# A fourth weight buffer, a planner that plans in rounds, and the odd pairs' activations turned by transfers

## The chip, the cores and the metric

The kernel runs on one core of one Trainium2 chip. The metric is the device time of one execution in microseconds (us). The engines are PE (TensorE), DVE (VectorE), ACT (ScalarE), POOL (GpSimd) and SP (SyncE), which here only issues transfers.

## The reference

A decoder trunk of two layers on 256 tokens of width 2048, in float32. Layer 0 is a retention layer, layer 1 latent attention; each is followed by a squared-ReLU MLP of inner width 8192. The change touches the MLPs.

```python
def sq_relu_mlp(h, w1, w2):
    return jnp.square(jax.nn.relu(h @ w1)) @ w2

for layer in range(DEPTH):
    if layer < N_A_LAYERS:
        x = x + retention(rms_norm(x, norm_mix[layer]), ...)
    else:
        ...
        x = x + mla_attention(rms_norm(x, norm_mix[layer]), ...)
    x = x + sq_relu_mlp(rms_norm(x, norm_mlp[layer]), mlp_w1[layer], mlp_w2[layer])
```

## The kernel before

**Products.** Each float32 operand is split into a high part in the type float32r and the rest, a low part. ACT casts the high part (wh), DVE subtracts for the low one (wl), and a product takes three matmuls: high by high, high by low, low by high. `gemm_pair` makes a 256 x 1024 block of output from chunks of 256 rows of weights, 1 MB each: SP loads a chunk into a buffer raw (tag "raw", three of them), `quad` splits it. A chunk is of one of two kinds. With eight block products it takes 24 matmuls and two splits of 1024 elements. With seven, the saving by sums of blocks, it takes 21, and DVE makes sums of weights (u) first and then splits of 1024, 512, 1024 and 1024 elements. Which chunks have seven stands in tuples such as ODD = (1, 3, 5, 7); chunks of one pair are numbered 0 to 7. The results stand in PSUM as c11, c12, c21, c22 and, for the seven kind, p1, p5, p6, p7; `pair_out` copies and adds them.

**The MLP.** In `mlp` the inner width is cut into four groups. A group has two up pairs p (even, then odd; names u_20 to u_27 and u_30 to u_37 are the chunks of pairs 2 and 3) and two down pairs (d_100 to d_107 and d_110 to d_117 in group 1). An up pair gives 1024 inner activations of 256 tokens, which a down pair needs with the inner width on the partitions: they must be turned. For an even pair `turn_by_dma` does it: ACT copies the 16-bit halves apart (hid_h), SP issues four transposing transfers for each 512 columns (hid_t), ACT copies the halves together (hid_u), squares and casts. For an odd pair, where STEPS holds None, `turn_on_pe` does it: PE transposes 128 x 128 blocks against the identity into PSUM (hid_tp), and ACT squares from there. The first four blocks of a down pair's eight come from the even pair, the last four (hid_30 to hid_33 in group 1) from the odd one. Three of the four groups' down results are added to memory by accumulating transfers that POOL issues (`to_home`, x_home or xh).

**The order.** Nothing is issued as it is written. `Plan` records every operation with its cost (`time`), takes due dates from the end backwards (`due_dates`), and `schedule` places the operations forwards, on each engine the ready one that is due first, with the buffers of each tag as a resource. Queues of an engine are in order: an instruction that waits holds up all behind it. All records go through one line, L421, so the trace tells operations apart by tiles.

Of the kernel before, what the change touches and what calls it, by code (L numbers as in the profile page):

```python
# [11 lines left out]
F32 = mybir.dt.float32  # L12
# [9 lines left out]

AHEAD = {"f2k": 25000, "act": 30000, "small": 60000}
COPY = {128: 160, 256: 269, 384: 370, 512: 490, 640: 625, 768: 735, 1024: 952}
SCALED = {64: 220, 128: 292, 256: 365, 384: 468, 512: 588, 1024: 1070}
# [97 lines left out]
class Plan:  # L125
# [60 lines left out]
    def time(self, op, outs, ins):  # L186
        engine, (_, method) = op.engine, op.method
        n = max(v.index.size for v in outs if isinstance(v, View)) if any(isinstance(v, View) for v in outs) else 0
        m = max([n] + [v.index.size for v in ins])
        op.moves = None  # L190
        if "dma" in method:
            size = max(n, m) * P * (2 if "transpose" in method else 4)
            issue = {"SP": 380, "ACT": 100, "POOL": 870}[engine]
            if "transpose" in method:
                issue = 1290
            rate, wait = (208, 3200) if op.kw.get("accum_op") is not None else (349, 3000 if engine == "POOL" else 1800)
            if "transpose" in method:
                rate, wait = 180, 2200
            op.moves = (size / rate, wait)
            return issue, issue  # L200
        if engine == "PE":
            if method == "matmul" and ins[0].dtype == F32:
                return 1.68 * n, 1.68 * n + 160
            cost = max(109, n / 2.4 + 13.5) if method == "matmul" else 109
            if method == "matmul" and ins[0].dtype == BF16:
                cost = 427
            return cost, cost + 165
        if engine == "DVE":
            base = 129 if method == "scalar_tensor_tensor" else 69
            return base + 1.0417 * m, base + 85 + 1.0417 * m  # L210
        if engine == "ACT":
            plain = method == "copy"
            cost = between(COPY if plain else SCALED, m)
            if plain and outs[0].dtype == U16 and m == 512:
                cost = 632
            if method == "activation" and op.kw.get("accum_out") is not None:
                return cost + 40, cost + 60
            return cost, cost + 115
        if op.kw.get("op") == ALU.pow:
            return 1050 + 75 * n, 1050 + 75 * n  # L220
        if method == "tensor_tensor":
            return 560 + 1.5 * m, 560 + 1.5 * m
        return 450 + 2.8 * m, 450 + 2.8 * m
# [28 lines left out]
            if not op.after:  # L252
                op.due = -whole

    def schedule(self):
        import heapq

        self.due_dates()
        free = dict.fromkeys(self.LATENCY, 0.0)
        server = 0.0  # L260
        waiting = {e: [] for e in free}
        ready = {e: [] for e in free}
        slots = {t: [(0.0, i) for i in range(b[0].bufs)] for t, b in self.tags.items()}
        turn, taken, held = ({t: k() for t in self.tags} for k in (int, set, set))
        chain = [op for op in self.ops if op.engine == "PE"]
        front = [0, False]
        blocked = {t: {} for t in self.tags}
        for op in self.ops:
            op.behind = {o for o in op.behind if o.number not in op.before}
            for other in op.behind:  # L270
                other.ahead.append(op)
            op.left, op.ready, op.start = len(op.before) + len(op.behind), 0.0, None
# [55 lines left out]
        while True:  # L328
            best = None
# [133 lines left out]
TURNED_Y = 7  # L463
TURNED_X = (0,1)
TURNED_CQ = (0,1)
STEPS = (((3,3,4),(3,4,5)),(None,None))
TURNS = ((0,1),(0,1))
SEVEN, LATE, ODD, HEAD = (3, 5, 7), (5, 7), (1, 3, 5, 7), (2, 4, 6, 7)
QUERY, FOUR = (3, 4, 6, 7), (3, 5, 6, 7)
# [18 lines left out]
def yoco(ctx: ExitStack, tc: tile.TileContext, a):  # L488
# [3 lines left out]
    psum = ctx.enter_context(tc.tile_pool(name="ps", bufs=1, space=PSUM))  # L492

    def f2k(shape, name, dtype=F32):
        return nc.tile(pool, [P, *shape], dtype, name, "f2k", 14)

    def small(w, name):
        return nc.tile(few, [P, w], F32, name, "small", 36)
# [182 lines left out]

    def stream(w, chunk, cols, name, use, done=None, before=None):

        raw = nc.tile(pool, [P, 2048], F32, f"{name}_raw", "raw", 3)
        if before is None:
            nc.sync.dma_start(raw[:, :cols], w[chunk])
        n = cols // 2
        for half in range(2):
            wh = nc.tile(pool, [P, 1024], F32R, f"{name}_wh{half}", "wh", 5)
            wl = nc.tile(pool, [P, 1024], F32R, f"{name}_wl{half}", "wl", 5)  # L690
            cuts = 1
            if before is not None:
                cuts = 1 if half and chunk else 2
                m = n // cuts
                for i in range(cuts):
                    lo = half * n + i * m
                    nc.sync.dma_start(raw[:, lo : lo + m], w[chunk][:, lo : lo + m])
                    if i == 0:
                        before(half)
            m = n // cuts  # L700
            for i in range(cuts):
                lo = half * n + i * m
                low_part[0] = split(wh[:, i * m : (i + 1) * m], wl[:, i * m : (i + 1) * m], raw[:, lo : lo + m])
            use(half, wh, wl)
            if half and done is not None:
                queue.append((clock[0] + 0.5, -1, done))
            tick(0.5)
# [47 lines left out]

    def quad(w, chunk, x, mm, name, split_ends=False):

        raw = nc.tile(pool, [P, 2048], F32, f"{name}_raw", "raw", 3)
        nc.sync.dma_start(raw, w[chunk])
        v, more = x  # L760

        def a(t, k):
            return [v[:, k, i, t * P : (t + 1) * P] for i in range(2)]

        def s(n):
            return [more[:, n // 2, i, n % 2 * P : (n % 2 + 1) * P] for i in range(2)]

        def parts(src, n, part):
            wh = nc.tile(pool, [P, 1024], F32R, f"{name}_wh{part}", "wh", 5)
            wl = nc.tile(pool, [P, 1024], F32R, f"{name}_wl{part}", "wl", 5)  # L770
            low_part[0] = split(wh[:, : n * 512], wl[:, : n * 512], src)
            return [[i[:, j * 512 : (j + 1) * 512] for i in (wh, wl)] for j in range(n)]

        if more is None:
            b11, b22 = parts(raw[:, 0:1024], 2, 0)
            if not split_ends:
                mm("c11", a(0, 0), b11)
                mm("c21", a(1, 0), b11)
                mm("c12", a(0, 1), b22)
                mm("c22", a(1, 1), b22)  # L780
            b12, b21 = parts(raw[:, 1024:], 2, 1)
            if split_ends:
                for key, ks in (("c11", ((0, 0, b11), (0, 1, b21))), ("c21", ((1, 0, b11), (1, 1, b21))),
                                ("c12", ((0, 1, b22), (0, 0, b12))), ("c22", ((1, 1, b22), (1, 0, b12)))):
                    for t, k, b in ks:
                        mm(key, a(t, k), b)
                return
            mm("c11", a(0, 1), b21)
            mm("c21", a(1, 1), b21)
            mm("c12", a(0, 0), b12)  # L790
            mm("c22", a(1, 0), b12)
            return
        u = [nc.tile(pool, [P, 2, 512], F32, f"{name}_u{i}", "us", 2) for i in range(2)]
        nc.vector.tensor_tensor(
            u[0], raw[:, 0:1024].rearrange("p (i n) -> p i n", i=2),
            raw[:, 1024:1536].unsqueeze(1).to_broadcast([P, 2, 512]), op=ALU.add,
        )
        nc.vector.tensor_tensor(u[1][:, 0], u[0][:, 0], raw[:, 512:1024], op=ALU.add)
        nc.vector.tensor_tensor(u[1][:, 1], u[1][:, 0], raw[:, 1536:], op=ALU.add)
        b11, b22 = parts(raw[:, 0:1024], 2, 0)  # L800
        mm("p1", a(0, 0), b11)
        mm("c12", s(3), b22)
        (b21,) = parts(raw[:, 1536:], 1, 1)
        mm("c11", a(0, 1), b21)
        u2, u4 = parts(u[1].rearrange("p i n -> p (i n)"), 2, 2)
        mm("c21", a(1, 1), u4)
        mm("p6", s(2), u2)
        u1, u3 = parts(u[0].rearrange("p i n -> p (i n)"), 2, 3)
        mm("p5", s(1), u1)
        mm("p7", s(0), u3)  # L810
# [485 lines left out]
    def mlp(layer, act, r, done):  # L1296
        w1, w2 = a[f"mlp_w1_{layer}"], a[f"mlp_w2_{layer}"]
        f0 = 0
        for gi, nf in enumerate(GROUPS):
# [46 lines left out]
            for p in range(f0 // 2, (f0 + nf) // 2):  # L1346
                seven = (ODD, ODD)[p % 2] if p else LATE
                gemm_pair(
                    w1, p * 8, act, [i in seven for i in range(8)], f"u{layer}_{p}", lambda c, p=p, up=up: up(c, p)
                )  # L1350
            if last:
                x_tiles(f"mlp{layer}")
            for p in range(2):
# [15 lines left out]
                    into_x(done, c, p, 1) if last else to_home(c, p)  # L1369

                kinds = [i in ((LATE if last else (SEVEN, ODD)[1]) if p else (SEVEN, ODD)[0]) for i in range(2 * nf)]
                gemm_pair(w2, p * 32 + 2 * f0, blocks, kinds, f"d{layer}_{gi}{p}", add)
            f0 += nf

    ss = square_sums(NB, "ss2")
# [379 lines left out]
```

## Time and profile before

| | us |
|---|---|
| median of 3 runs | 2434.55 (2434.27 to 2435.98) |
| profiled execution, whole | 2433.66 |
| its span | 2431.9 |
| PE busy in the span | 2415.1 |
| DVE busy | 2228.8 |
| ACT busy | 1764.0 |

The profile is one execution. A matmul's duration is its way through the array, and matmuls overlap: the distance between starts is what one costs PE. The same holds in a small way for DVE and ACT, where an operation starts a little before the one ahead of it ends. In the rows below, x with a number counts instructions, and names leave out buffer numbers: hid_tp stands for all transposes of hidden activations, u_wh and d_wh for the high parts of up and down weights.

### The profile page before, as it was taken

The page shows a single profiled execution, that of the slowest core. Times are in us where ns is not written, and L with a number is a line of the kernel's source. Part 1 is how long each engine was busy: PE and PEld are TensorE (multiplying, and loading weights), DVE is VectorE, ACT ScalarE, POOL GpSimd, SP SyncE. Part 2 cuts the span into 40 slices and gives each one's busy share as a digit, 9 for nine tenths or more (in the row PEclk, how much of TensorE's full clock was granted, in tenths as well). Part 3 has the DMA queues.
Part 4 walks back from the last instruction along what each step waited for, and adds up shares of the span by engine and source line. Part 5 has one row for each costly group of instructions (what it writes and reads, how often), then busy time and mean ns, then how long its engine had stood idle before and what let it go on. Part 6 is the DMA issues. An engine that isn't in the chain of part 4 may idle for free.

```text
span 2431.9 us, 31709 instructions
## 1 busy us (share of the span) xinstructions
PE 2415.1 (99%) x11342; PEld 2027.4 (83%) x11342; DVE 2228.8 (92%) x2959; ACT 1764.0 (73%) x2505; POOL 251.7 (10%) x287
## 2 busy tenths in 40 slices
PE   9999999999999999999999999999999999999998
PEld 7888888888888888888888888998888888888877
DVE  6899999988999999999999998777899999899999
ACT  6667666666687858769668879677878587596694
POOL 6510001000000010010110001110000100100100
PEclk9999999999999999999999999999999999999999
DMA  9566669656675697696896766545766986977984
GB/s 341 179 212 201 201 199 257 216 190 220 217 239 209 206 258 236 211 260 221 237 279 211 222 216 200 169 140 188 218 219 197 256 239 208 256 227 220 270 230 160
DMA packets 161151, 537.33 MB, mean 221 GB/s; under 512 B 78560, under 2 KB 79968, under 8 KB 107744
## 3 DMA queue, kind: packets, MB, share of 16 engines
q1 hardware_dynamic: 139600, 489.09, 60.9%
q0 software_dynamic: 21248, 46.15, 9.6%
q8 instruction: 89, 1.46, 0.2%
q14 instruction: 70, 0.57, 0.1%
q10 hardware_dynamic: 144, 0.05, 0.0%
HBM read 479.14 MB, written 39.85 MB: 213 GB/s over the span
## 4 chain that ended last, share of the span: by engine, by line
PE 76%; DVE 13%; ACT 5%; issue 4%; DMA 3%; SPq 0%; DVEq 0%; ACTq 0%
PE u_c L421 14%; PE d_c L421 12%; PE rp_c L421 8%; PE ro_c L421 5%; DVE d_wl L421 5%; PE u_p L421 4%; PE uq_acc L421 4%; PE rq_acc L421 4%; PE rk_acc L421 4%; PE d_p L421 3%; PE rp_p L421 3%; DVE d_u L421 2%; PE ku_acc L421 2%; DMA u_raw<-in_mlp_w 2%; DVE u_wl L421 2%
## 5 line engine op out<-in xcount | busy, mean ns | idle before, releaser
L421 PE MATMUL d_c<-d_wh,hid 128*128 128x512 f32 x1412 | 456.3, 390 | 0.0
L421 PE MATMUL u_c<-u_wh,n 128*128 128x512 f32 x1328 | 429.6, 389 | 0.0
L421 PEld LDWEIGHTS d_c<-d_wh,hid 128*128 128x128 f32 x1412 | 265.0, 188 | 54.6
L421 PEld LDWEIGHTS u_c<-u_wh,n 128*128 128x128 f32 x1328 | 249.3, 188 | 51.6
L421 DVE TENSOR_TENSOR d_wl<-d_raw,d_wh 128x1024 fp32r<-128x1024 f32 (+1 forms) x256 | 279.3, 1106 | 0.2 <-ACT d_wh L421 0.2
L421 ACT CAST u_wh<-u_raw 128x1024 fp32r<-128x1024 f32 (+1 forms) x256 | 236.6, 953 | 53.8 <-PE u_c L421 37.3
L421 PE MATMUL d_c<-d_wl,hid 128*128 128x512 f32 x706 | 274.8, 389 | 0.0
L421 DVE TENSOR_TENSOR u_wl<-u_raw,u_wh 128x1024 fp32r<-128x1024 f32 (+1 forms) x256 | 273.6, 1093 | 1.2 <-ACT u_wh L421 1.2
L421 PE MATMUL u_c<-u_wl,n 128*128 128x512 f32 x664 | 258.8, 390 | 2.6 <-DVE u_wl L421 2.5
L421 ACT CAST d_wh<-d_raw 128x1024 fp32r<-128x1024 f32 (+1 forms) x256 | 240.9, 967 | 19.9 <-PE d_c L421 8.0
L421 ACT CAST d_wh<-d_u 128x1024 fp32r<-128x1024 f32 x106 | 108.8, 1051 | 146.9 <-DVE d_u L421 139.4
L421 ACT CAST u_wh<-u_u 128x1024 fp32r<-128x1024 f32 x120 | 122.4, 1051 | 103.3 <-DVE u_u L421 93.5
L421 PE MATMUL rp_c<-rp_wh,a 128*128 128x512 f32 x560 | 180.8, 390 | 0.0
L421 PEld LDWEIGHTS d_c<-d_wl,hid 128*128 128x128 f32 x706 | 132.6, 188 | 27.2
L421 DVE TENSOR_TENSOR u_wl<-u_u,u_wh 128x1024 fp32r<-128x1024 f32 x120 | 143.1, 1219 | 12.3 <-ACT u_wh L421 12.3
L421 PEld LDWEIGHTS u_c<-u_wl,n 128*128 128x128 f32 x664 | 124.6, 188 | 30.0 <-DVE u_wl L421 4.3
L421 ACT CAST rp_wh<-rp_raw 128x1024 fp32r<-128x1024 f32 x112 | 103.7, 944 | 59.2 <-PE rp_c L421 33.4
L421 DVE TENSOR_TENSOR d_wl<-d_u,d_wh 128x1024 fp32r<-128x1024 f32 x106 | 126.9, 1218 | 14.5 <-ACT d_wh L421 14.3
L421 DVE TENSOR_TENSOR rp_wl<-rp_raw,rp_wh 128x1024 fp32r<-128x1024 f32 x112 | 119.4, 1092 | 6.3 <-ACT rp_wh L421 6.3
L421 PEld LDWEIGHTS rp_c<-rp_wh,a 128*128 128x128 f32 x560 | 105.1, 188 | 22.7 <-DVE rk_u L421 1.1
L421 PE MATMUL u_p<-u_wh,n_more 128*128 128x512 f32 x360 | 120.6, 389 | 0.0
L421 POOL DMA_DIRECT2D xh<-d_c x48 | 41.6, 866 | 736.8 <-DVE d_wl L421 536.1
(492 smaller groups left out, 6029.4 us busy)
## 6 DMA issues: line engine op xcount, KB each, us to landing
u_raw<-in_mlp_w SPq DMA_DIRECT2D x128, 1024.0 KB, 6.4
d_raw<-in_mlp_w SPq DMA_DIRECT2D x128, 1024.0 KB, 5.2
rp_raw<-in_ret_w_gv SPq DMA_DIRECT2D x56, 1024.0 KB, 5.1
ro_raw<-in_ret_w_out SPq DMA_DIRECT2D x32, 1024.0 KB, 5.1
uq_raw<-in_mla_w_uq SPq DMA_DIRECT2D x24, 768.0 KB, 4.1
rq_raw<-in_ret_w_qk SPq DMA_DIRECT2D x16, 1024.0 KB, 5.9
rk_raw<-in_ret_w_qk SPq DMA_DIRECT2D x16, 1024.0 KB, 4.9
xh<-d_c POOLq DMA_DIRECT2D x48, 256.0 KB, 6.2
```

Source lines behind the costliest of these rows:

```text
L421: op.made = fn(*(real(v) for v in op.args), **{k: real(v) for k, v in op.kw.items()})
```

## The change

Seven things change. The tag raw gets four buffers, f2k sixteen of 2 KB per partition; the room comes from the scratch for descriptors of POOL's transfers, which goes from 16 KB (the default) to 4 KB a partition. STEPS gives the odd pairs the even pairs' way, so `turn_on_pe` is not used any more. All up pairs take their chunks in the order 0 to 5, 7, 6, and the last one (6, of eight products) closes c11, c21, c12 and c22 one after another (`ends`). The planner's costs for transfers are longer. `schedule` runs the forward pass, now `forward`, up to six times; after each, `latest` computes new due dates from the end backwards with each engine's own order as a limit, and the plan with the earliest planned end is kept. At the start, buffers count as free 1 us earlier.

```diff
+ROUNDS = 6
-            rate, wait = (208, 3200) if op.kw.get("accum_op") is not None else (349, 3000 if engine == "POOL" else 1800)
+            rate, wait = (150, 3200) if op.kw.get("accum_op") is not None else (330, 2600)
             if "transpose" in method:
-                rate, wait = 180, 2200
+                rate, wait = 180, 3000
+    def latest(self):
...
+        while True:
...
+            op = heapq.heappop(ready[e])[2] if ready[e] else heapq.heappop(waiting[e])[3]
+            op.due = free[e] = min(limit[op], free[e] - op.cost)
...
     def schedule(self):
+        self.due_dates()
+        best = None
+        for _ in range(ROUNDS):
+            try:
+                self.forward()
...
+            end = max(op.end for op in self.ops)
+            if best is None or end < best[0]:
+                best = (end, [(op.start, [b.slot for b in op.new]) for op in self.ops])
+            self.latest()
...
-        slots = {t: [(0.0, i) for i in range(b[0].bufs)] for t, b in self.tags.items()}
+        slots = {t: [(-1000.0, i) for i in range(b[0].bufs)] for t, b in self.tags.items()}
...
-STEPS = (((3,3,4),(3,4,5)),(None,None))
+STEPS = (((3,3,4),(3,4,5)),((3,3,4),(3,4,5)))
...
-        return nc.tile(pool, [P, *shape], dtype, name, "f2k", 14)
+        return nc.tile(pool, [P, *shape], dtype, name, "f2k", 16)
...
-        raw = nc.tile(pool, [P, 2048], F32, f"{name}_raw", "raw", 3)
+        raw = nc.tile(pool, [P, 2048], F32, f"{name}_raw", "raw", 4)
...
-                    w1, p * 8, act, [i in seven for i in range(8)], f"u{layer}_{p}", lambda c, p=p, up=up: up(c, p)
+                    w1, p * 8, act, [i in seven for i in range(8)], f"u{layer}_{p}", lambda c, p=p, up=up: up(c, p),
+                    **(({"order": (0, 1, 2, 3, 4, 5, 7, 6), "ends": True}, {"order": (0, 1, 2, 3, 4, 5, 7, 6), "ends": True}))[p % 2],
...
-    nc = bacc.Bacc("TRN2", target_bir_lowering=False, num_devices=1)
+    nc = bacc.Bacc("TRN2", target_bir_lowering=False, num_devices=1, dynamic_dma_scratch_size=4096)
```

In all, PE has 128 operations fewer (the transposes); DVE and POOL have the same ones; ACT has 96 more, all copies (32 into halves, 64 out of them), and its 32 squares from PSUM become squares in place; SP has 64 transposing transfers more.

PE in group 1 of layer 0: the end of chunk d_100 and the start of d_101. Before:

```order
L421 MATMUL d_10_c_8962<-d_100_wl_8921,hid_20_8825 128x512
L421 MATMUL d_10_c_8962<-d_100_wh_8911,hid_20_8825 128x512
L421 MATMUL hid_30_tp<-cst,u_3_c_8918 128x128
L421 MATMUL hid_30_tp<-cst,u_3_c_8925 128x128
L421 MATMUL hid_30_tp<-cst,u_3_c_8918 128x128
L421 MATMUL hid_30_tp<-cst,u_3_c_8925 128x128
L421 MATMUL hid_31_tp<-cst,u_3_c_8918 128x128
L421 MATMUL hid_31_tp<-cst,u_3_c_8925 128x128
L421 MATMUL hid_31_tp<-cst,u_3_c_8918 128x128
L421 MATMUL hid_31_tp<-cst,u_3_c_8925 128x128
L421 MATMUL d_10_c_8939<-d_101_wh_8941,hid_21_8891 128x512
L421 MATMUL d_10_c_8939<-d_101_wl_8964,hid_21_8891 128x512
```

And after:

```order
L480 MATMUL d_10_c_8998<-d_100_wh_8912,hid_20_8800 128x512
L480 MATMUL d_10_c_8998<-d_100_wl_8934,hid_20_8800 128x512
L480 MATMUL d_10_c_8998<-d_100_wh_8912,hid_20_8800 128x512
L480 MATMUL d_10_c_8973<-d_101_wh_8926,hid_21_8804 128x512
L480 MATMUL d_10_c_8973<-d_101_wl_8964,hid_21_8804 128x512
```

The batch of eight transposes is gone; the matmuls around it stand as they stood.

SP at the same place, where the loads of weights and the transposing transfers share one queue. Before:

```order
L421 DMA u_36_raw<-in_mlp_w_0 128x2048
L421 DMA_TRANSPOSE hid_20_t_8705<-hid_20_h_8694 128x4x128
L421 DMA_TRANSPOSE hid_20_t_8705<-hid_20_h_8702 128x4x128
L421 DMA_TRANSPOSE hid_20_t_8730<-hid_20_h_8694 128x4x128
L421 DMA_TRANSPOSE hid_20_t_8730<-hid_20_h_8702 128x4x128
L421 DMA u_37_raw<-in_mlp_w_0 128x2048
L421 DMA d_100_raw<-in_mlp_w_0 128x2048
L421 DMA d_101_raw<-in_mlp_w_0 128x2048
L421 DMA_TRANSPOSE hid_21_t_8859<-hid_21_h_8847 128x4x128
L421 DMA_TRANSPOSE hid_21_t_8859<-hid_21_h_8856 128x4x128
L421 DMA d_102_raw<-in_mlp_w_0 128x2048
L421 DMA_TRANSPOSE hid_21_t_8885<-hid_21_h_8847 128x4x128
```

And after:

```order
L480 DMA d_100_raw<-in_mlp_w_0 128x2048
L480 DMA d_101_raw<-in_mlp_w_0 128x2048
L480 DMA d_102_raw<-in_mlp_w_0 128x2048
L480 DMA d_103_raw<-in_mlp_w_0 128x2048
L480 DMA d_104_raw<-in_mlp_w_0 128x2048
L480 DMA_TRANSPOSE hid_30_t_8996<-hid_30_h_8984 128x4x128
L480 DMA_TRANSPOSE hid_30_t_9011<-hid_30_h_8984 128x4x128
L480 DMA_TRANSPOSE hid_30_t_8996<-hid_30_h_9005 128x4x128
L480 DMA_TRANSPOSE hid_30_t_9011<-hid_30_h_9005 128x4x128
L480 DMA d_105_raw<-in_mlp_w_0 128x2048
L480 DMA d_106_raw<-in_mlp_w_0 128x2048
L480 DMA d_107_raw<-in_mlp_w_0 128x2048
```

The even pair's transfers (hid_20, hid_21) have moved ahead of d_100; the odd pair's (hid_30) stand between the loads d_104 and d_105.

ACT after, from the first copy of the odd pair into halves to the first copies out of them; before, nothing of the odd pair but its squares from hid_tp stood here:

```order
L480 COPY hid_30_h_8984<-u_3_c_8940 128x1024
L480 CAST d_101_wh_8993<-d_101_raw 128x1024
L480 COPY hid_30_h_9005<-u_3_c_8953 128x1024
L480 CAST d_102_wh_9015<-d_102_raw 128x1024
L480 CAST d_102_wh_9023<-d_102_raw 128x1024
L480 CAST d_103_wh_9032<-d_103_raw 128x1024
L480 CAST hid_23_more<-hid_23_sum 128x2x256
L480 CAST d_103_wh_9059<-d_103_raw 128x512
L480 COPY hid_30_u<-hid_30_t_8996 128x512
L480 COPY hid_31_u<-hid_30_t_8996 128x512
L480 ACTIVATE u_3_c_8967<-u_3_c_8967,n_r 128x512
L480 CAST d_103_wh_9083<-d_103_u_9002 128x1024
```

The copy hid_30_u waits for two of the transfers above, and the casts of d_103 behind it wait with it. The cast of hid_30, which PE needs for chunk d_104, stands eleven instructions further on.

## Rows read from the trace of the kernel before

**Rows 1.** The page's first part: busy us, share of the span, instructions by engine.
```profile
PE 2415.1 (99%) x11342; PEld 2027.4 (83%) x11342; DVE 2228.8 (92%) x2959; ACT 1764.0 (73%) x2505; POOL 251.7 (10%) x287
```

**Rows 2.** Windows: length, busy PE, PEld, DVE, ACT, POOL (x), PEclk, DMA share, GB/s.
```profile
885.31:1051.01 165.70, 165.70 (x740) 137.35 (x740) 159.82 (x188) 122.35 (x159) 13.82 (x17) 1.00 0.78 235
...
1921.81:2087.00 165.19, 164.12 (x731) 135.20 (x730) 158.27 (x187) 120.44 (x155) 13.73 (x16) 1.00 0.79 235
```

**Rows 3.** PE in time around a batch of transposes: start us, us, operation, out<-in.
```profile
806.26 0.39 PE L421 MATMUL d_c<-d_wh,hid 128*128 128x512 f32 x1
806.49 1.03 PE L421 MATMUL hid_tp<-cst,u_c 128*128 128x128 f32 x8
807.28 0.48 PE L421 MATMUL d_c<-d_wh,hid 128*128 128x512 f32 x1
807.60 0.40 PE L421 MATMUL d_c<-d_wl,hid 128*128 128x512 f32 x1
```

**Rows 4.** The page's groups by line and form: the transposes of the hidden activations.
```profile
L421 PE MATMUL hid_tp<-cst,u_c 128*128 128x128 f32 x128 | 17.5, 274 | 1.5 <-ACT u_c L421 1.5
```

**Rows 5.** What PE and its weight loads (PEld) waited for: us, times, longest.
```profile
PE u_c L421 <- DVE u_wl L421: 2.5, 2, 2.1
...
PEld u_c L421 <- DVE u_wl L421: 4.3, 4, 2.6
PEld hid_tp L421 <- ACT u_c L421: 2.9, 4, 1.2
```

**Rows 6.** The same for DVE and ACT, two of their waits in the up pairs.
```profile
ACT u_wh L421 <- PE u_c L421: 45.3, 58, 1.7
...
DVE u_u L421 <- DMA u_raw<-in_mlp_w: 12.4, 15, 2.2
```

**Rows 7.** The chain that ended last, near PE's longest wait: start us, us, what.
```profile
2308.42 7.59 DMA u_raw<-in_mlp_w
```

**Rows 8.** The same chain in layer 0: two chunks that follow each other.
```profile
885.31 5.44 PE u_c L421 x24
895.51 5.44 PE u_c L421 x24
```

**Rows 9.** Groups by line and form on ACT: busy, mean ns, idle before and releaser.
```profile
L421 ACT CAST d_wh<-d_u 128x1024 fp32r<-128x1024 f32 x106 | 108.8, 1051 | 146.9 <-DVE d_u L421 139.4 <-DVE hid_sum L421 5.2 <-PE d_c L421 1.8
...
L421 ACT COPY hid_u<-hid_t 128x512 uint16<-128x512 uint16 x64 | 48.7, 779 | 4.8 <-DMA hid_t<-hid_h 4.8
...
L421 ACT CAST d_wh<-d_raw 128x512 fp32r<-128x512 f32 x53 | 33.0, 623 | 0.3 <-PE d_c L421 0.3
...
L421 ACT COPY hid_h<-u_c 128x1024 uint16<-128x1024 uint16 x32 | 32.1, 1038 | 0.1
```

**Rows 10.** DMA issues: times, KB each, median us from issue to landing.
```profile
xh<-d_c POOLq DMA_DIRECT2D x48, 256.0 KB, 6.2
...
hid_t<-hid_h SPq DMA_TRANSPOSE x64, 3.4
...
y_t<-y_h SPq DMA_TRANSPOSE x28, 5.8
```

**Rows 11.** Busy time by windows around the start of a down pair, layer 0.
```profile
1112.00:1132.00 20.00, 20.00 (x90) 16.53 (x90) 19.03 (x24) 18.93 (x26) 0.00 (x0) 1.00 0.76 230
1132.00:1153.00 21.00, 21.00 (x102) 17.56 (x101) 20.48 (x29) 20.90 (x33) 0.00 (x0) 1.00 0.67 216
1153.00:1173.00 20.00, 20.00 (x90) 16.56 (x89) 20.00 (x28) 13.07 (x17) 0.00 (x0) 1.00 0.50 174
```

**Rows 12.** DVE's instructions in time, operations of 1024 elements in a row.
```profile
1007.60 2.36 DVE L421 TENSOR_TENSOR d_wl<-d_raw,d_wh 128x1024 fp32r<-128x1024 f32 x2
1009.87 1.22 DVE L421 TENSOR_TENSOR d_u<-d_raw 128x1024 f32<-128x1024 f32 x1
```

**Rows 13.** ACT's instructions in time, two casts in a row.
```profile
1054.44 2.00 ACT L421 CAST u_wh<-u_u 128x1024 fp32r<-128x1024 f32 x2 [1.68 <-DVE u_u L421]
```

**Rows 14.** SP's queue in time, four transposing transfers in a row.
```profile
1107.68 5.12 SPq L421 DMA_TRANSPOSE hid_t<-hid_h  x4
```

More of the change, by code (lines that the diff above doesn't have):

```diff
@@ L253, in due_dates @@
                 op.due = -whole
-    def schedule(self):
+    def latest(self):
+        import heapq
+        left = {op: len(op.after) for op in self.ops}
+        behind = {op: [] for op in self.ops}
+        limit, free = {}, dict.fromkeys(self.LATENCY, 0.0)
+        waiting = {e: [] for e in free}
+        ready = {e: [] for e in free}
+        for op in self.ops:
+            for other, finish in op.after:
+                behind[other].append((op, finish))
+            limit[op] = -(op.took if op.moves is None else op.cost + sum(op.moves))
+            if not op.after:
+                heapq.heappush(waiting[op.engine], (-limit[op], -op.start, op.number, op))
+        while True:
+            best = None
+            for e in free:
+                w, r = waiting[e], ready[e]
+                while w and -w[0][0] >= free[e] - w[0][3].cost:
+                    heapq.heappush(r, heapq.heappop(w)[1:])
+                at = free[e] if r else -w[0][0] if w else None
+                if at is not None and (best is None or at > best[0]):
+                    best = (at, e)
+            if best is None:
+                break
+            e = best[1]
+            op = heapq.heappop(ready[e])[2] if ready[e] else heapq.heappop(waiting[e])[3]
+            op.due = free[e] = min(limit[op], free[e] - op.cost)
+            for other, finish in behind[op]:
+                gap = other.cost
+                if finish and not other.engine == op.engine == "PE":
+                    gap = (other.took if other.moves is None else gap + sum(other.moves)) + self.LATENCY[op.engine]
+                limit[other] = min(limit[other], op.due - gap)
+                left[other] -= 1
+                if not left[other]:
+                    heapq.heappush(waiting[other.engine], (-limit[other], -other.start, other.number, other))
@@ new lines, in schedule @@
+    def schedule(self):
+        self.due_dates()
+        best = None
+        for _ in range(ROUNDS):
+            try:
+                self.forward()
+            except RuntimeError:
+                if best is None:
+                    raise
+                break
+            end = max(op.end for op in self.ops)
+            if best is None or end < best[0]:
+                best = (end, [(op.start, [b.slot for b in op.new]) for op in self.ops])
+            self.latest()
+        for op, (start, slots) in zip(self.ops, best[1]):
+            op.start = start
+            for buf, slot in zip(op.new, slots):
+                buf.slot = slot
+        return sorted(self.ops, key=lambda op: (op.start, op.number))
@@ L256, in schedule, with forward @@
+    def forward(self):
         import heapq
-        self.due_dates()
         free = dict.fromkeys(self.LATENCY, 0.0)
@@ L267, in schedule @@
         blocked = {t: {} for t in self.tags}
+        for op in self.ops:
+            op.ahead = []
         for op in self.ops:
@@ L1371, in mlp @@
                 kinds = [i in ((LATE if last else (SEVEN, ODD)[1]) if p else (SEVEN, ODD)[0]) for i in range(2 * nf)]
-                gemm_pair(w2, p * 32 + 2 * f0, blocks, kinds, f"d{layer}_{gi}{p}", add)
+                gemm_pair(w2, p * 32 + 2 * f0, blocks, kinds, f"d{layer}_{gi}{p}", add, **(({}, {}))[p % 2])
             f0 += nf
```

2 lines of the change are left out of this document (1 added, 1 removed).

## The prediction

> **What bounds the kernel now.** I read the page's first part, then a table by stage, then what PE itself waits for. In the first, PE is busy in 99% of the span, DVE in 92%, ACT in 73% [rows 1]. The table by stage shows one group of an MLP in each layer, about 165 us long, both at a granted clock of 1.00, the 2.4 GHz level: in layer 0 PE is busy for 165.70 of 165.70 us and DVE for 159.82; in layer 1 PE misses 1.1 us [rows 2]. So time goes down only where PE has fewer instructions or where one of its few waits goes, and DVE is close behind: 5.9 us of room in a group.
>
> **The 128 transposes that leave PE.** The hidden activations of the odd pairs (four a layer) are turned on PE, 16 a pair in two batches of eight. The reader should look at starts, not at durations: the batch starts at 806.49, 0.23 us after the matmul before it, the matmul after it at 807.28 and the next only at 807.60 [rows 3]. Up to 807.60 these are 1.11 us, of which one matmul's own step is 0.23: a batch costs 0.88 us, 0.11 a transpose. 16 batches: 14.1 us off PE. In the new order PE goes straight from chunk d_100 to d_101, and the counts of the other matmuls stay.
> The grouped row gives a transpose a mean duration of 274 ns [rows 4]. The Trainium skill (TensorE: Matmul & The Clock Gate, Part 4: PE-mode transpose) has about 275 ns for one inside a kernel, and the trace agrees on the duration. Taken as a cost, that would be 128 x 0.274 = 35 us; the starts show that the transposes overlap, so the sum goes by 14.1.
>
> **Waits that go with them.** Before its transposes PE waited for the scaled activations: 1.5 us on the matmul side [rows 4], 2.9 on the weight-load side [rows 5]. I take the middle, 2.2. The activations are now waited for by ACT and SP, and what is late next is the turned block (below).
>
> **The fourth weight buffer.** PE waited for u_wl for 2.5 us, 4.3 by its loads [rows 5]. The chain shows the origin of the largest: with three buffers a load is issued when DVE lets go of one, and lands 7.59 us later [rows 7]; DVE waited for u_raw 15 times, 12.4 us in all [rows 6]. With a fourth buffer a load is issued one chunk, about 5 us of PE, earlier: 5.44 us for a chunk of 24 matmuls, and 10.20 - 5.44 = 4.76 for one of 21 [rows 8]. 7.6 us of landing then fit into the lead. I take 3.4 us (the middle of 2.5 and 4.3), and that the 12.4 us come back as room on DVE. The bounds are 0 and 4.3.
> The smaller descriptor scratch I cost at nothing. POOL's accumulating transfers come in runs of eight, and one lands after 6.2 us [rows 10]. If each had to wait for the landing of the one before, a run would take 8 x 6.2 = 50 us, still within a group's 165; only f2k buffers are held longer, of which there are two more. Above nothing there is no price that reaches PE, below nothing neither.
>
> **What is added.** 64 transposing transfers on SP, and on ACT 32 copies into halves and 64 copies out of them: 32 x 1.038 + 64 x 0.779 = 83 us [rows 9], 10.4 a group. On ACT's total (122 of 165 us in a group, rows 2) that is hidden. The place where it may not be is the start of a down pair: there ACT is busy for 20.90 of 21 us already, and for 13 of 20 in the stretch behind [rows 11]. The new plan answers in two ways that the order shows: the even pair's transfers are issued ahead of the odd pair's last chunks, so that its copies are over before d_100; and every up pair now ends with chunk 6, of eight products, which closes its sums one after another, while the sums p are closed a chunk earlier.
> The step that must hold: hid_30, the odd pair's first block, is read by chunk d_104. From the end of u_36 PE works for 3 x 5.44 + 4.76 = 21.1 us on d_100 to d_103 [rows 8]. In that time ACT has, from the first hid_30_h to the cast of hid_30, 23 instructions in the new order: 8 casts of 1.05 us, 4 copies of 1.04, 4 of 0.78, and 7 more of 512 elements, all taken at the 0.62 of the cast of that size [rows 9]: 20.0 us by durations. Two casts in a row take 2.00 and not 2.10 [rows 13], so 22 overlaps of 0.1 make it 17.8. With 0.7 us ahead of it for the copy of the last sum it is 18.5 to 20.7 against 21.1.
> The wait inside it: between the second hid_30_h and the first copy out stand three casts of 1024 and two of 512, about 4.0 us with their overlaps. SP needs 5.12 us to issue four transposes [rows 14], so the third is issued some 0.6 us after that hid_30_h, and lands 3.4 us after issue [rows 10]: at 4.0, just in time. At the 5.8 us of the retention's y_t [rows 10] ACT would stand for 2.4 us, with the weight casts of d_103 and d_104 queued behind it, and DVE and PE behind those. Bounds a group: 0, and 20.7 + 2.4 - 21.1 = 2.0; over eight groups 0 to 16 us. hid_t's own row is the nearer one, so I take 0.4 a group, 3.4 us. SP's d_105 load stands behind the four transposes, 5.1 us late; three loads are ahead of it, so it is hidden; without the fourth buffer DVE would wait for it.
> The added transfers carry 128 KB each, 8.4 MB, under 2% of the bytes. They fall where the queues have room: a share of 0.67 and then 0.50 from the start of a down pair on [rows 11].
> The Trainium skill (DMA: Bandwidth & Descriptors, Specifications) asks for pieces of at least 512 B for line rate, and more short pieces speak against the change. The trace shows something of it, a share of 0.76 at 230 GB/s with transposes against 0.50 at 174 without [rows 11].
>
> **The sum.** The profiled execution took 2433.66 us, 1.8 around a span of 2431.9. 2433.66 - 14.1 - 2.2 - 3.4 + 3.4 = 2417.4. The median of the runs shown, 2434.55, is 0.9 above the profiled one: 2418.
>
> **Rivals.**
> *The turned block comes late (A).* Transfers land as the retention's do, and each down pair stalls for 1 to 2 us: 8 to 16 us instead of 3.4, so 2423 to 2431. For it speaks an ACT almost without a gap at that place today [rows 11]; against it the 3.4 us of hid_t's landing, and that ACT waited for hid_t for only 4.8 us in all 64 copies [rows 9].
> *Two sevens in a row starve PE (B, slower).* The up pairs now end with chunks 5, 7, 6, of which 5 and 7 are of the seven-product kind. For such a chunk DVE does four operations of 1024 and three of 512 elements; two of 1024 are followed by the next after 2.27 us, a step of 1.14 [rows 12], and a 512 is estimated at half of it: 6.3 us of DVE against 4.76 of PE. Alternating, each deficit of 1.5 is made up by the next eight-product chunk (2.3 against 5.44); in a row it is 3.0, and the stock must cover it. If it is not there, each of 16 up pairs loses 1.5 us more: 24 us, so 2418 - 3.4 + 24 = 2439. It decides from 1.2 us a pair on. Against it: ACT found all its high-part buffers full 58 times in the up pairs, waiting for PE [rows 6], so there is a stock of five half chunks; and DVE gets the 12.4 us of rows 6 back.
> *Only the transposes count (C).* The buffer brings nothing and the new waits eat the rest: 2434.55 - 14.1 = 2420, within the forecast's own range.
> *More comes out (D).* No new wait at all, and the re-planned retention part loses its few waits too: 2434.55 - 14.1 - 2.9 - 4.3, and 1 to 3 for those waits: 2410 to 2412.
>
> **How the numbers follow.** The forecast with C, 2412 to 2423: 0.62. D, below 2412: 0.10. A, 2423 to 2431: 0.18. B: 0.10. A measurement of this kernel tells a change of 0.2%, 4.9 us, from none, so faster ends at 2429.7. A gives 0.12 to faster and 0.06 to the same; B, whose price runs from nothing to 24, 0.03 to the same and 0.07 to slower. That is 0.84, 0.09 and 0.07; for a mishap in the re-planned rest of the kernel, which I cannot price, I move 0.02 from faster to the other two: 0.82, 0.10 and 0.08. The range that holds 8 of 10 reaches from D's middle to most of A: 2409 to 2430.
>
> **What the new profile would show.** No hid_tp on PE, and 11,214 matmuls or so. hid_t with 128 transfers at about 3.4 us. In a group of layer 0 PE busy throughout, and a group of about 164 us instead of 165.7. DVE's wait for u_raw far under 12.4 us. The step on ACT is wrong if PE or DVE wait for a d_wh or hid cast at d_103 to d_105; B is right if PE waits for u_wl in chunks 7 and 6. I am wrong altogether if PE's idle time grows by more than 14 us.

## The result, and the profile after

The changed kernel takes 2447.5 us (median of 4 runs, 2446.3 to 2449.9), the kernel before 2435.3 beside it: ratio 1.0044, 95% interval 1.0031 to 1.0057. It is slower by about 12 us, where 2418 was forecast.

Page of the changed kernel, first part (busy us, share of the span, instructions), beside [rows 1]:

```profile
span 2445.5 us, 31624 instructions
PE 2426.7 (99%) x11214; PEld 2016.6 (82%) x11214; DVE 2247.5 (92%) x2959; ACT 1843.0 (75%) x2601; POOL 262.7 (11%) x287
```

The 128 transposes are gone from PE, ACT has 79 us more, and the span is 13.6 us longer. The first place to look is a stretch in which PE never stops. Windows of the changed kernel (columns as in [rows 2]; a line of dots stands for lines left out):

```profile
885.31:1051.01 165.70, 165.70 (x725) 135.70 (x724) 161.98 (x190) 132.35 (x171) 13.84 (x16) 1.00 0.85 241
...
800.00:1000.00 200.00, 200.00 (x873) 163.69 (x873) 194.57 (x231) 167.41 (x222) 13.89 (x16) 1.00 0.84 241
...
1112.00:1132.00 20.00, 20.00 (x88) 16.35 (x88) 19.82 (x24) 19.77 (x27) 0.00 (x0) 1.00 0.80 235
1258.00:1281.00 23.00, 21.15 (x93) 16.95 (x91) 15.99 (x21) 13.56 (x18) 2.81 (x6) 1.00 1.14 276
...
1281.50:1286.00 4.50, 3.66 (x9) 2.68 (x10) 4.40 (x5) 4.50 (x7) 0.00 (x0) 0.67 0.98 350
```

In the first row's 165.70 us the kernel before did 740 matmuls, 16 of them transposes [rows 2]; now 725 matmuls without a transpose fill the same 165.70 us, at the same granted clock of 1.00. So a group is not shorter, though work left it and PE did not wait. The second row says why: 200 us without idle time hold 873 matmuls, 229 ns each. Call the distance from the start of a matmul to the start of PE's next instruction its step. Worked out from the starts of all 512-column matmuls with steps under 300 ns, the mean step was 227.4 ns before (9331 steps) and is 229.9 now (9336). That is 9336 x 2.48 = 23.2 us, spread over the whole span.

What PE, DVE and ACT wait for in the changed kernel (us in total, times, longest), beside [rows 5, 6]:

```profile
PE d_c L480 <- ACT hid L480: 3.1, 2, 2.3
PE u_c L480 <- DVE u_wl L480: 2.9, 4, 0.8
PE u_c L480 <- ACT u_wh L480: 2.4, 1, 2.4
...
ACT hid_u L480 <- DMA hid_t<-hid_h: 12.9, 3, 7.7
```

DVE's 12.4 us for u_raw [rows 6] do not occur any more. In their place ACT stands for turned blocks for 12.9 us (4.8 before, [rows 9]), 7.7 us in one piece, and PE has waits for ACT that [rows 5] did not show. DMA issues of the changed kernel (count, KB, median us to landing), beside [rows 10]; the kernel before had for x_mlp, the tiles of x that the last groups read back, the row under it:

```profile
xh<-d_c POOLq DMA_DIRECT2D x48, 256.0 KB, 5.8
x_mlp<-xh POOLq DMA_DIRECT2D x16, 256.0 KB, 12.8
hid_t<-hid_h SPq DMA_TRANSPOSE x128, 3.8
```

```profile
x_mlp<-xh POOLq DMA_DIRECT2D x16, 256.0 KB, 4.9
```

The landing of all hid_t, before and after:

```profile
DMA to landing us min/median/max: 2.4/3.4/6.9
```

```profile
DMA to landing us min/median/max: 2.4/3.8/13.1
```

The median of hid_t has hardly moved; its longest landing has, from 6.9 to 13.1 us. The longest ACT wait lies in layer 0's last group. Timelines of the changed kernel, ACT and then PE (start us, us, what, idle time before and its releaser):

```profile
1271.17 1.04 ACT L480 COPY hid_h<-u_c 128x1024 uint16<-128x1024 uint16 x1
1279.87 0.76 ACT L480 COPY hid_u<-hid_t 128x512 uint16<-128x512 uint16 x1 [7.65 <-DMA hid_t<-hid_h]
1280.50 1.98 ACT L480 CAST u_wh<-u_u 128x1024 fp32r<-128x1024 f32 x2
```

```profile
1278.52 0.39 PE L480 MATMUL u_c<-u_wl,n 128*128 128x512 f32 x1
1278.75 0.40 PE L480 MATMUL u_c<-u_wh,n 128*128 128x512 f32 x1
1281.58 0.50 PE L480 MATMUL u_c<-u_wh,n 128*128 128x512 f32 x1 [2.44 <-ACT u_wh L480]
1282.84 0.67 PE L480 MATMUL u_c<-u_wl,n 128*128 128x512 f32 x1 [0.76 <-DVE u_wl L480]
1283.31 0.63 PE L480 MATMUL u_c<-u_wh,n 128*128 128x512 f32 x1
1283.74 0.63 PE L480 MATMUL u_p<-u_wh,n_more 128*128 128x512 f32 x1
```

ACT stands at the copy of a turned block; the weight cast behind it comes 7.65 us late, DVE's low part after it, PE stops for 2.44 and 0.76 us. Then the matmuls start 0.43 us apart instead of 0.23: the window 1281.5 to 1286 above has a granted clock of 0.67, between the 2.4 GHz level that PE had before it stood and 1.2 GHz; by 1287 it is 1.00 again.

By starts, first matmul to last: 128-column matmuls -15.2 us, 512-column steps under 300 ns +24.3 (23.2 by their length, 1.1 for five more of them), steps of 300 ns and more (the stalls) +4.6, the rest, shorter matmuls, +1.2: +15 us in all. The stalls are thus the smaller part.

### The profile page after: what moved, and what is told of

The parts are those of the page before. It is cut to its first block, busy times and chain, and to the rows that moved or that the text cites. A ratio compares the mean times of both kernels' runs of the same rounds, so it can differ in the third digit from the quotient of the medians.

```text
span 2445.5 us, 31624 instructions
## 1 busy us (share of the span) xinstructions
PE 2426.7 (99%) x11214; PEld 2016.6 (82%) x11214; DVE 2247.5 (92%) x2959; ACT 1843.0 (75%) x2601; POOL 262.7 (11%) x287
## 4 chain that ended last, share of the span: by engine, by line
PE 89%; ACT 4%; DVE 3%; DMA 2%; issue 1%; POOL 0%; SPq 0%; ACTq 0%; DVEq 0%; POOLq 0%
PE d_c L480 20%; PE u_c L480 17%; PE rp_c L480 9%; PE u_p L480 6%; PE d_p L480 6%; PE ro_c L480 6%; PE uq_acc L480 4%; PE rq_acc L480 3%; PE rk_acc L480 3%; PE rp_p L480 3%; PE ku_acc L480 2%; PE wo_acc L480 1%; PE ro_p L480 1%; PE dqp_c L480 1%; PE dq_acc L480 1%
```

## The experiments

**Where tiles lie.** The new plan moves more than the instructions the diff speaks of. SP issues the load of the table cst at 0.7 us before and at 12.3 us now:

```profile
L421 SPq DMA_DIRECT2D cst<-in_cst x1: 400/400/400, 0.7 to 0.7; - x1
```

```profile
L480 SPq DMA_DIRECT2D cst<-in_cst x1: 328/328/328, 12.3 to 12.3; - x1
```

The trace holds no addresses; those below are worked out from the programs. Tiles get their addresses in SBUF, the memory on the chip, in the order in which the plan first uses them. cst takes 2688 bytes of a partition, 10 x 256 + 128. Before, it lies ahead of all rings, and every weight and activation tile begins 192 bytes past a multiple of 256. Now three raw buffers, the first weight buffers wh0, wl0 and wh1, and an activation tile lie ahead of it and begin at 64; the others behind it at 192. The steps of the changed kernel go by buffer: products from wh0/wl0 take 232.2 ns, from the last two pairs of weight buffers under 229.

*cst first.* The changed kernel, same plan, with two tiles created before the others:

```diff
     with self.tc.manual_schedule(engines=engines):
+        for v in self.first:            # gains, cst
+            v.get()
```

> The changed kernel, with one tile (the table cst, 2688 B per partition) placed in SBUF ahead of the others again, as it lies in the kernel before; no instruction and no order changes, only addresses: every weight tile then begins 192 bytes past a multiple of 256, where in the changed kernel wh0, wl0 and wh1 begin 64 past one. Theory P (placement): the 512-column matmuls go back from 229.9 to about 227 ns from start to start, 9336 x 2.5 ns = 23 us less: 2424 us, ratio to the kernel before about 0.9955. Rival T (the added transposing transfers and ScalarE copies slow TensorE's reads everywhere): nothing changes, 2447 us, ratio 1.004.

2430.7 us, ratio to the kernel before 0.9966 (95% interval 0.9954 to 0.9977; so in all runs below). 882 matmuls in the same 200 us, 226.8 ns each. Windows of this run:

```profile
800.00:1000.00 200.00, 200.00 (x882) 164.95 (x882) 196.00 (x237) 168.29 (x223) 13.89 (x16) 1.00 0.83 239
```

By ratio it is 19 us faster than the changed kernel, between the profiled spans 16, and not 23: its stalls (of each step over 1.4 times the median of its size, what lies above the median, all added) are 40.1 us against 31.1. With the same plan, a faster PE waits longer for the others. Theory P holds, T falls.

*The mixture in the kernel before.* The first buffers of each ring, up to the second wh, are created ahead of cst in the kernel before:

```diff
     with self.tc.manual_schedule(engines=engines):
+        self.first[0].get()             # gains
+        seen = set()
+        for op in order:
+            for buf in op.new:
+                if buf.tag in ("raw", "f2k", "act", "wh", "wl", "us", "junk") \
+                        and (buf.tag, buf.slot) not in seen \
+                        and sum(t == "wh" for t, _ in seen) < 2:
+                    seen.add((buf.tag, buf.slot))
+                    buf.get()
```

> The kernel before, with the first buffers of the ring tags placed ahead of the table cst, up to the second wh buffer, so that wh0, wl0 and wh1 begin 64 bytes past a multiple of 256 and all other weight tiles 192 past one, as in the changed kernel; order and instructions are those of before. Theory P: the 512-column matmuls go from 227.4 to about 229.9 ns, +23 us: 2458 us, ratio 1.0095. Rival T: no change, 2435 us, ratio 1.000.

2454.0 us, ratio 1.0065 (1.0053 to 1.0077); the step goes from 227.4 to 230.0 ns. The same stretch of the same order, before and in this run:

```profile
800.00:1000.00 200.00, 200.00 (x900) 165.92 (x899) 193.59 (x233) 153.24 (x203) 13.86 (x16) 1.00 0.75 228
```

```profile
800.00:1000.00 200.00, 200.00 (x889) 163.88 (x888) 191.04 (x230) 154.93 (x206) 13.86 (x16) 1.00 0.75 228
```

The placement alone makes the kernel before slower than the changed one is. Of the 24 us that the steps add, 19.9 show between the profiled spans: stalls and the waits at the transposes are shorter in turn (stalls 21.8 us against 27.0). The ratio, of the medians of several runs, shows 15.8.

*All tiles at 64.* As above, for all rings of the changed kernel, cst behind them.

> The changed kernel with the table cst placed behind all ring buffers, so that every weight and activation tile begins 64 bytes past a multiple of 256. Theory P in the form that the offset itself is slow: all 512-column matmuls at the 232.7 ns of the changed kernel's wh0/wl0 pair, 9336 x 5.3 ns = 50 us above an undisturbed run, about 2474 us, ratio 1.016. Theory P in the form that only a mixture of offsets is slow: 2424 us, ratio 0.9955. Rival T: 2447 us, ratio 1.004.

2428.1 us, ratio 0.9962 (0.9950 to 0.9975), step 227.5 ns; in the same stretch:

```profile
800.00:1000.00 200.00, 199.93 (x880) 164.57 (x879) 195.65 (x235) 167.17 (x221) 13.89 (x16) 1.00 0.85 238
```

The offset 64 is not slow; only a mixture is.

*Activations apart from weights.* The 24 activation tiles ahead of cst (64), all weight tiles behind it (192).

> The changed kernel with its 24 activation tiles placed ahead of the table cst and all weight tiles behind it: activations (stationary) begin 64 bytes past a multiple of 256, weights (moving) 192 past one, none otherwise. Theory P2 (a matmul is slow where its moving and its stationary tile differ in that offset; where the moving tiles were at 192 and the stationary ones at 64 for 13 matmuls running, the trace shows 233.0 ns, against 226.7 where both agree): about 9300 matmuls at 233.0 in place of 226.7 ns, +58 us on the run with cst first, 2489 us, ratio 1.021. Rival P1 (only a mixture among the weight tiles, between high and low parts or between buffers, is slow): 2431 us, ratio 0.997.

2468.3 us, ratio 1.0126 (1.0107 to 1.0145). Windows of this run:

```profile
800.00:1000.00 200.00, 200.00 (x863) 162.15 (x862) 192.64 (x228) 165.28 (x215) 13.91 (x16) 1.00 0.79 235
```

863 matmuls; over the run the step is 232.4 ns, 5.0 more than with cst first, 46 us, of which 9.4 come back in shorter stalls. No two weight tiles differ here, so P1 falls: what counts is whether a matmul's moving tile (the weights, 128x512) and its stationary tile (the activations, 128x128, loaded by PEld) agree in the offset. P2 had 58 us for it, on 6.3 ns a matmul.

**Why stalls eat the turning.** With the placement mended, 13 us more stalls than before are left (40.1 against 27.0), in the last groups of both layers and the first of layer 1.

*The old order of the up pairs' chunks*, with cst first:

```diff
-    **({"order": (0, 1, 2, 3, 4, 5, 7, 6), "ends": True}, ...)[p % 2],
```

> The run with cst first, and besides the up pairs' chunks in their old order (0 to 7, ends not split). Theory P with the new order harmless: within 2 us of the run with cst first (2424). Rival B of the prediction (two seven-product chunks in a row starve TensorE): below the run with cst first by up to 24 us, 1.5 us for each of 16 pairs. Rival T: 2447 us or, with B, less.

2434.5 us, ratio 0.9985 (0.9976 to 0.9994), 4.6 us slower than the new order, which rival B held to be the loss. What PE waits for in this run:

```profile
PE d_c L482 <- ACT hid L482: 13.5, 9, 2.2
```

This is the wait that the prediction feared, in each of the eight groups. With the new order it is 3.3 us, 2 times.

*Three raw buffers*, with cst first: `"raw", 4` to `"raw", 3`.

> The run with cst first, with three raw weight buffers in place of four. Theory Q (the transposing transfers queue behind one weight transfer more; ScalarE stands for hid_t 6.4 and 7.1 us in the last groups of both layers and the weight casts stand behind it): latest landing of hid_t back from 13.2 us towards the 6.9 us of the kernel before, the ScalarE waits go, about 8 us less than cst first: 2422 us. Rival R3 (the fourth buffer is what keeps weights in time, as the prediction credited it): 3 to 6 us more than cst first, 2434 to 2437 us.

2433.1 us, ratio 0.9982 (0.9972 to 0.9991): slower than cst first by 4 us. The latest landing falls to 9.5 us and ACT's waits for hid_t to 3.5 in all, as Q has it, but PE's waits for u_wl rise from 2.6 to 5.4, and DVE waits 6.7 us for u_raw again. Both mechanisms are there; R3 is the larger.

*The last up pair of each layer on PE*, with cst first: `if p != 7 else None` behind `STEPS[p % 2][i]`.

> The run with cst first, with the inner activations of the last up pair of each layer (p = 7) turned on TensorE again: 32 transposes, 4 batches of 0.88 us = 3.5 us more of TensorE. Theory A (rival A of the prediction: a turned block that lands late holds ScalarE and the casts behind it): the stalls at 1268 to 1275 us and 2311 to 2323 us go (4.8 + 8.4 - 2.9 us), so some 7 us less net: 2424 us. Rival (the stalls there have another cause, such as the new order of the chunks): 3.5 us more, 2434 us.

2419.5 us, ratio 0.9928 (0.9914 to 0.9941), 9 us below cst first: faster than both kernels. The stalls of the last groups are nearly gone (1.8 and 0.6 us for 4.7 and 8.4). But the block awaited there is the *even* pair's (p = 6), turned by transfers before the change too; so it is not the turning of p = 7 itself that is awaited. What else the new plan moves is shown under the x tiles below.

*A later landing in the plan*, with cst first: transposing transfers planned at 8000 ns in place of 3000.

> The run with cst first, with the planner told that a transposing transfer lands 8.0 us after its share of the queue, in place of 3.0, so that what reads it is planned later. Theory A (readers are planned before the transfer has landed, and ScalarE stands): the ScalarE waits of 6.4 and 7.1 us for hid_t shrink, up to 8 us less than cst first: 2423 us. Rival: the plan's order is bound by buffers and not by that cost, 2431 us, or by the f2k buffers held longer, more.

2425.8 us, ratio 0.9953 (0.9939 to 0.9968). ACT's wait for hid_t with cst first, and in this run:

```profile
ACT hid_u L482 <- DMA hid_t<-hid_h: 13.5, 2, 7.1
```

```profile
ACT hid_u L482 <- DMA hid_t<-hid_h: 1.1, 1, 1.1
```

The longest landing is still 11.9 us: a late landing costs where the order makes ACT stand for it. But PE's waits for hid rise from 3.3 to 7.6 us, so only a part comes back.

*Both cures:*

> The run with p = 7 on TensorE, and besides the planner told of 8.0 us for a transposing transfer's landing. If the two cures act on the same stalls (the last groups' hid_t): within 1.5 us of the run with p = 7 on TensorE, 2418 to 2421 us. If they act on different ones: up to 5 us less, 2414 us.

2422.4 us, ratio 0.9940 (0.9926 to 0.9954): no better than p = 7 on PE alone (0.9928), so the two act largely on the same stalls.

*The x tiles.* POOL's timeline in the changed kernel, and in the kernel before, where the last groups begin:

```profile
1256.14 3.58 POOL L480 DMA_DIRECT2D x_mlp<-xh  x6
1267.01 1.14 POOL L480 DMA_DIRECT2D x_mlp<-xh  x2 [7.28 <-PE u_c L480]
```

```profile
1253.92 1.46 POOL L421 DMA_DIRECT2D x_mlp<-xh  x2
1263.24 1.07 POOL L421 DMA_DIRECT2D x_mlp<-xh  x2 [7.86 <-PE u_c L421]
1268.01 1.06 POOL L421 DMA_DIRECT2D x_mlp<-xh  x2 [3.69 <-PE u_p L421]
1273.44 1.06 POOL L421 DMA_DIRECT2D x_mlp<-xh  x2 [4.38 <-PE u_c L421]
```

Six loads issued in 3.6 us in the new plan, two at a time before. The run with p = 7 on PE has spread them again, and hid_t lands after 9.2 us at most there:

```profile
1245.63 1.47 POOL L482 DMA_DIRECT2D x_mlp<-xh  x2
...
1261.04 1.07 POOL L482 DMA_DIRECT2D x_mlp<-xh  x2 [3.50 <-PE u_p L482]
1266.48 1.14 POOL L482 DMA_DIRECT2D x_mlp<-xh  x2 [4.37 <-PE u_c L482]
```

The run with cst first, same plan, with these loads replaced by a fill with zeros when the instructions are issued, so that the loads and their part of the result are left out:

```diff
+if method == "dma_start" and op.args[0].__class__ is View and op.args[0].buf.name.startswith("x_mlp"):
+    op.made = self.nc.gpsimd.memset(real(op.args[0]), 0.0)
+    continue
```

> The run with cst first, same plan and order, with the 16 loads of x_mlp (256 KB each, issued by GpSimd in the last group of each layer) replaced by a GpSimd fill with zeros of the same tiles; the loads and so their part of the result are left out. Theory X (in the last groups six of these loads go out within 3 us beside the weights, the queues are full, the turned block of the even pair lands after 12 to 13 us, ScalarE stands for it and the weight casts stand behind it): latest landing of hid_t from 13.2 us to below 8, ScalarE's 6.4 and 7.1 us for hid_t gone, TensorE's stalls at 1268 to 1275 and 2311 to 2323 us (4.8 + 8.4 us) gone: about 2419 us. Rival Y (the weights alone, with four raw buffers, delay it): within 3 us of the run with cst first, 2428 to 2431 us.

2417.3 us, ratio 0.9922 (0.9908 to 0.9936). The stretch at the same times as above (DMA share 1.14 there) and the landing of hid_t around it, from 1240 to 1285 us, in this run:

```profile
1258.00:1281.00 23.00, 23.00 (x103) 19.03 (x102) 22.88 (x28) 22.45 (x31) 0.34 (x1) 1.00 0.86 233
```

```profile
DMA to landing us min/median/max: 2.5/3.5/5.0
```

In the changed kernel that line, for the same times, reads:

```profile
DMA to landing us min/median/max: 7.6/10.3/13.1
```

In this stretch ACT has no wait for hid_t left (1.1 us in the whole run), and PE is busy throughout. This run is ahead of the changed kernel by then; from 1248 to 1271 us its DMA share is 0.98, still under 1.14. X holds: the loads of the x tiles delay the turned block. That it is their burst, and not that they are there, is argued from the kernel before and the run with p = 7 on PE, which have the same loads, spread, and short stalls there.

**The parts alone.** *The turning alone*, in the kernel before (`STEPS`, both parities by transfers):

> The kernel before with one part of the change alone: the odd up pairs' inner activations turned by transfers too (128 transposes off TensorE); three raw buffers, full descriptor scratch, the old planner and its costs, all weight tiles at the offset of before. The prediction's first term: -14.1 us and -2.2 us of waits, 2419 us, ratio 0.993, if the added 10.5 us of ScalarE per group and the late transfers cost nothing; theory A: it gives back what the run with cst first gives back (13 us), about 2432 us.

2467.7 us, ratio 1.0125 (1.0106 to 1.0144), worse than either theory. Its waits on PE:

```profile
PE d_c L423 <- ACT hid L423: 16.8, 11, 1.9
PE u_c L423 <- DVE u_wl L423: 5.6, 3, 2.9
PE d_p L423 <- ACT hid L423: 3.9, 8, 0.5
```

*Everything but the turning*, with cst first (`STEPS[1]` back to None, so that the odd pairs are turned on PE):

> The run with cst first, with all odd up pairs' activations turned on TensorE as in the kernel before (128 transposes in 16 batches): every other part of the change, without the turning by transfers. Theory A (the turning takes 14.1 us off TensorE and gives back about 10 to 13 us in stalls at its landing): within 4 us of the run with cst first, 2427 to 2435 us, with the ScalarE waits for hid_t of the last groups gone. Rival (the planner, the fourth buffer and the new order alone carry a gain, and the turning is a loss): 2422 us or less.

2426.6 us, ratio 0.9957 (0.9942 to 0.9971). Stalls 20.3 us against 40.1, 128-column matmuls 12.8 us more: turning all the odd pairs is worth nothing here. Turning all but the last one of each layer (0.9928, above) is 7 us better than this.

*Scratch alone; scratch and buffers; planner alone*, in the kernel before:

> The kernel before with the descriptor scratch of 4096 bytes alone; all tiles move down by 12288 bytes, which leaves their offset to a multiple of 256 as it was. The prediction's zero for the smaller scratch: ratio 1.000, within 0.2%. Rival (GpSimd waits for room for descriptors, and its x tiles and sums arrive late): slower by more than 5 us.

> The kernel before with the smaller scratch, a fourth raw buffer and 16 in place of 14 f2k buffers; planner, costs, order and the turning as before, weight tiles at the offset of before. The prediction's third term: 3.4 us less, ratio 0.9986 (TensorE's 2.1 us wait for u_wl and the late u_raw gone). If the gain of the run with all odd pairs on TensorE (ratio 0.996) lies in the buffers: 10 us less, 0.996.

> The kernel before with the planner in six rounds and its new transfer costs alone; three raw and 14 f2k buffers, full scratch, the turning and the order of the chunks as before, weight tiles at the offset of before. The prediction gave the planner no time of its own: ratio 1.000. If the gain of the run with all odd pairs on TensorE lies in the planner: up to 10 us less, 0.996.

Ratios 1.0011 (1.0001 to 1.0021), 0.9970 (0.9958 to 0.9982) and 0.9944 (0.9931 to 0.9956). The planner alone (with the buffers free 1 us earlier) gains most, 13.6 us. The gains do not add: planner, buffers and the order of the chunks together (0.9957, above) gain less than the planner alone. All three lower the same small sum of stalls, from 27.0 us to 23.0 with the buffers, 17.1 with the planner, 20.3 with all; that this is the reason is argued.

*Which pairs to turn.* On the run with p = 7 on PE, besides layer 1's p = 1; and, on cst first, p = 1 and 7 of both layers:

> The run with p = 7 on TensorE, and besides layer 1's p = 1 on TensorE (16 transposes, 1.8 us). What is left of stalls there, 6.8 us from 1800 to 1900 us (u_wl, and d_c for hid 2.4 us with half-speed matmuls behind it), comes by theory A from ScalarE's pile of turning work in that group: 3 to 5 us of it go, net 1 to 3 us less than the run with p = 7 on TensorE: 2417 us. Rival (the pile there comes from the stage before the layer): 1.8 us more, 2421 us.

> The run with cst first, with the odd pairs of the first and the last group of both layers (p = 1 and 7, 64 of the 128 transposes) turned on TensorE again, and only those of the two inner groups by transfers. If the stalls belong to these groups alone: those of 1200 to 1300, 1800 to 1900 and 2300 to 2400 us go (4.8 + 6.9 + 8.4 us) for 7 us of transposes, about 2417 us, ratio 0.992. If the plan moves them into other groups: 2421 us or more.

2419.6 us, ratio 0.9930 (0.9916 to 0.9944), level with p = 7 alone; and 2421.2, 0.9943 (0.9930 to 0.9955). In the latter the stalls of 1800 to 1900 and 2300 to 2400 us are about 3 us each, in place of 6.7 and 8.4: lower and not gone, and the transposes of p = 1 cost what they save.

## Why the prediction was wrong

- **The step that failed** is the sum itself, "2433.66 - 14.1 - 2.2 - 3.4 + 3.4": it holds what leaves PE and what PE waits for, and takes the step of the 11,214 matmuls that stay as unchanged. For the 512-column ones it grew by 1.1%, +23.2 us, because a table was loaded later and so placed elsewhere. None of the rivals had it, and the sign that was to tell "wrong altogether" could not show it: PE's idle time in the span went from 16.8 to 18.8 us only. With the mixture taken away, the kernel is faster than before (0.9966); with it put in, the kernel before becomes slower (1.0065).
- **The transposes and their waits**, 14.1 + 2.2: about right. 128-column matmuls with what they wait for fell by 15.2 us.
- **The fourth buffer**, 3.4: right, as far as one run tells. Taken from the run with cst first, it costs 4 us. In the kernel before, scratch, fourth buffer and the two f2k buffers together give 7.3 us. DVE's wait for u_raw is gone as foreseen.
- **The smaller scratch at nothing**: about right, +0.1% (0.01 to 0.21%).
- **New waits of 3.4 us at the start of down pairs**: right in mechanism, and only once at the place named: in layer 1's first group the chunk d_004 waits for the odd pair's first block, 2.3 us behind an ACT without a gap. With the old order of chunks all groups paid (13.5 us).
- **"They fall where the queues have room"**: wrong in the last groups. The stretch looked at was a middle group; in the last, the x tiles go out in a burst, the DMA share is 1.14 and hid_t lands after 13 us. Rival A had ACT standing and casts queued behind it, with 5.8 us for the landing and down pairs for the place; it is 10 to 13 us, at an up pair.
- **Rival B**: wrong. The new order gains 4.6 us.
- **The planner** had no term of its own. Alone it is worth 13.6 us.

With both causes taken away (cst first, no x loads) the ratio is 0.9922; the forecast was 2418 / 2434.55 = 0.9932. That they agree so closely is partly luck: the gains of the planner and of the new order, and the stalls left in layer 1's first group, stood nowhere in the sum, and the x loads are work that the kernel needs. Still open: what the 6.7 us of stalls in layer 1's first group come from beyond ACT's pile of work, and what spreading the x loads alone, with nothing else in the plan moved, would give.

## What to carry to other kernels

When a re-planned kernel is slower with its engine busy throughout, count instructions per window before looking for waits: fewer in the same busy time means that each takes longer, and the addresses of the operands are a suspect that no diff shows. Give tiles sizes, or an order of creation, that a plan cannot turn into different offsets. Read a transfer's landing time where all its neighbours run at once, the last group here, and let a moved step's price include the transfers that the plan bunches beside it.

## What was not expected of the hardware

A matmul of 512 columns steps at 226.9 to 227.1 ns where its moving and its stationary tile begin at the same offset to a multiple of 256 bytes in the partition, at 192 (226.9, 8700 steps of the run with cst first) as at 64 (227.1, 8698 steps of the run with cst last). Where they differ it steps at 232 to 234: at 232.5 with the moving tile at 192 and the stationary one at 64 (8697 steps of the run with activations apart), and at 233.4 with the moving tile at 64 and the stationary one at 192 (864 steps of the changed kernel; 233.6 over 948 steps of the kernel before with the mixture). In the latter case the steps alternate, 229 and then 237 to 238, so a single step tells little. Counted are steps under 300 ns in runs of at least 12 such matmuls with the same offsets, from the third on. In the two kernels with a mixture, runs that agree are not quite at the undisturbed figure (228.0 at 192 in the changed kernel), so a change of offsets reaches some matmuls beside it.

The granted clock is 1.00 in the stretches without idle time, at either step. The Trainium skill (SBUF — State Buffer, Operand start alignment) asks that an operand begin at a multiple of its element size, and says that this is about legality, not speed. All these tiles do so, and the measurement shows a price of speed beside that rule. Only these two offsets were tried; why they matter the runs do not show.
